# A two-layer trunk (RG-LRU, then forgetting attention): the values' bound taken from the weights, heads' operands loaded in pieces, projections reordered

## The chip, the core and the metric

The kernel runs on one core of a Trainium2 chip. A core has engines with a queue of instructions each, which run side by side and wait for one another by semaphores: TensorE (PE, matrix products; its weight loads are listed apart as PEld), VectorE (DVE), ScalarE (ACT), GpSimd (POOL) and SyncE (SP), which here only issues DMAs. The metric is the device time of one execution in microseconds.

## The reference

The input is x of 1024 tokens by 1024 channels. Two pre-norm residual layers and a final norm are computed, all in float32:

```
for i in range(2):
    h = rms_norm(x, norm_g[i])
    x = x + (lru_mixer if i == 0 else fox_mixer)(h, ...)
return rms_norm(x, final_g)

def fox_mixer(h, w_in, b_f, w_out):
    u = h @ w_in                       # q, k, v, gate: 16 heads of 64 each; f_logit: 16
    cum = cumsum(log_sigmoid(f_logit + b_f))
    logits = q @ k.T / 8 + (cum_q - cum_k), causal
    o = softmax(logits) @ v
    return (o * silu(gate)) @ w_out
```

`lru_mixer` is one product with w_in (1024 to 3072), a causal convolution over 4 tokens, two block-diagonal gates, a linear recurrence over the tokens, a SiLU gate and a product with w_out.

## The kernel before

Every product of projections takes float32 operands that are split into a high and a low part (`to_hi`, `to_lo`; `split_weights` does it for a block of weights: a load into `wf`, a cast to `wh`, a subtraction to `wl`), and runs as three matmuls: high by high, low by high, high by low. One "fill step" of a projection is six such matmuls.

The first layer runs over 12 blocks of 128 channels (loop over `n`, from line 395): per block the products with w_in, convolution, gates, recurrence; earlier blocks' output projection (`project_out`) fills in between. Lines 464 to 489 finish it: the last output projection, x written to DRAM (`x1d`), and the second norm's row sums (`rms_row`).

The second layer goes head by head. `values(g)` computes v for four heads at once (stages at g = 0, and in the runs of heads 3, 7 and 11): v is written as float16 in a high and a low part, and scaled into float16's range by a bound. `bound(g)` makes that bound: eight Squares on ACT of the weights' high parts and eight matmuls (`norms`) that sum them over the partitions, a maximum, a square root (which loads an ACT table), a reciprocal and the scales `rv`. The evacuation of v from PSUM (lines 583 and 584) uses `rv`; PSUM has two buffers for each of the tags "g", "O" and "S".

Per head, the 1024 queries are done in two chunks of 512 (c = 0, 1), and each chunk in four blocks of 128 (i). `maxima(hd, c)` yields once per block: logits S by two or four matmuls from T (keys) and U (queries), mask and row maximum on DVE, exp with row sum on ACT, the sums scaled by 1/TOP on POOL and inverted on DVE, weights in a high and a low part (`pp`, on ACT and DVE), and a DMA transpose of them to `pT`, issued by SP. `weigh(hd, c)` yields several times: O from `pT` and v.

T[s] (one tile of 1024 columns for each parity s of heads) and U are filled by DMAs on SP from the projected k and q (`load`, `load_q`): T in three large copies of 256 KB and a small one from `cumd`, U per chunk in three of 128 KB and a small one. U for c = 0 is one tile, `U0`, that all heads share.

`run(order, gens…)` writes the order out by hand: in the string, "1" is a block of `maxima`, "0" a step of `weigh`, "." a fill step of the projections for the next pair of heads (`kq_units`, `g_units`) or, for heads 12 on, of the output projection (`partial`, and then `turned`, the last part with the final norm), and each "." also advances `side`. For each head there are two runs: the first has `weigh(hd, 0)` with `maxima(hd, 1)`, the second `weigh(hd, 1)` with `maxima(hd + 1, 0)`. Heads 0 to 11 use `ORDER`, the others `LAST`. Each engine, and SP, works its queue in the order in which it was built.

Of the kernel before, what the change touches and what calls it, by code (L numbers as in the profile page):

```python
# [15 lines left out]
TOP = 32768.0  # L16
# [12 lines left out]
ORDER = "1.1.1.1..0.0", "1.1.1.1.0.00.0"  # L29
# [11 lines left out]
def trunk(ctx: ExitStack, tc: tile.TileContext, xt, w0, wg, wo0, pc, gn, gf, w1, wv, wf, bf, wo1, out):  # L41
# [11 lines left out]
    pe = [None]  # L53

# [17 lines left out]
    onesb = const.tile([P, P], BF16, name="onesb")  # L72
    nc.vector.memset(onesb, 1.0)
# [35 lines left out]
    def split_weights(src, shape, hi_eng, lo_eng, parts=wpool):  # L109
        wt = loaded(shape)  # L110
        for part, sl in src:
            nc.sync.dma_start(wt[:, :, sl], part)
# [73 lines left out]
    with ExitStack() as l0:  # L186
# [207 lines left out]

        ys, fill, held = [], iter(()), {}
        for n in range(NB):
# [66 lines left out]

        wl = [w for d0 in range(0, KT, 2) for w in out_weights(NB // 2 - 1, d0)]
        for h, cs in enumerate(halves):
# [23 lines left out]
            rms_row(sums, rs1[h], rms1[h])  # L489

# [6 lines left out]
    with ExitStack() as l1:  # L497
# [25 lines left out]
        def bound(g, parts):  # L523

            row = ps.tile([P, HALF], F32, tag="O", name="norms")[:, :256]
            for k in range(KT):
                sq = at.tile([P, 256], BF16, tag="yo", name="sqw", bufs=2)
                nc.scalar.activation(sq, f32(parts[k][0][:, :256]), AF.Square, scale=gnt[:, 1, k : k + 1])
                matmul(row, onesb, sq, start=k == 0, stop=k == KT - 1)
            most = const.tile([P, 1], F32, name=f"most{g}")  # L530
            nc.vector.tensor_reduce(most, row, mybir.AxisListType.X, ALU.max)
            nc.scalar.activation(most, most, AF.Sqrt, bias=tiny, scale=SEQ / TOP / TOP)
            unit_ = tops[g] = const.tile([P, 1], F32, name=f"unit{g}")
            nc.vector.tensor_scalar(unit_, most, 0.5 / TOP, None, ALU.mult)
            nc.vector.reciprocal(most, most)
            rv = const.tile([P, 8], F32, tag="rv", name="rv", bufs=2)
            for h in range(2):
                nc.vector.tensor_scalar(rv[:, 4 * h : 4 * h + 4], rms1[h], most, None, ALU.mult)
            return rv

        def values(g):
# [11 lines left out]
            rv = bound(g, parts)  # L553
# [5 lines left out]
            for st, k in todo:  # L559
# [19 lines left out]
                for a in range(2):  # L579
                    v = vpool.tile([P, 4, HD], FP16, tag=f"v{st}", name=f"v{st}", bufs=2)  # L580
                    src = pt[:, a * P : (a + 1) * P].rearrange("p (b d) -> p b d", b=2)
                    rv_ = rv[:, st : st + 1]
# [6 lines left out]
        tops = {}  # L589
# [8 lines left out]
        def low(pair):  # L598
            return nc.vector if pair else nc.gpsimd
# [24 lines left out]
        def load(hd, cs=slice(0, SEQ), us=(0, 1)):  # L624
# [4 lines left out]
            nc.sync.dma_start(f32(T[s][:64, 0, cs]), hi)  # L629
            nc.sync.dma_start(f32(T[s][:64, 1, cs]), hi)  # L630
            nc.sync.dma_start(f32(T[s][64:, 0, cs]), lo)
            nc.sync.dma_start(f32(T[s][66:68, 1, cs]), cumd[hd, :, cs])
            for c in us:
                load_q(hd, c)

        def load_q(hd, c):
# [3 lines left out]
            nc.sync.dma_start(f32(u[:64, 0]), hi)  # L640
            nc.sync.dma_start(f32(u[64:, 0]), hi)
            nc.sync.dma_start(f32(u[:64, 1]), lo)
            nc.sync.dma_start(f32(u[64:66, 1]), cumd[hd, :, halves[c]])
# [73 lines left out]
        def maxima(hd, c):  # L717
# [7 lines left out]
            for i in range(4 * c, 4 * c + 4):  # L725
# [6 lines left out]
                for lo_, hi_ in ((0, min(n, HALF - o_)), (HALF - o_, n)):  # L732
# [19 lines left out]
                nc.gpsimd.tensor_scalar(r, r, 1.0 / TOP, None, ALU.mult)  # L752
# [3 lines left out]
                nc.sync.dma_start_transpose(  # L756
                    turned_[:, : i + 1, :, qs].rearrange("p j t q -> p (j t) q"),
                    both.rearrange("p j t k -> p (j t k)"),
                )
                yield  # L760
        def weigh(hd, c, sub=slice(0, HALF)):
# [19 lines left out]
            to, one = yo[r0 : r0 + HD], tops[hd // 4]  # L781
# [4 lines left out]
        def gated(hd, c, sub=slice(0, HALF)):  # L786
# [10 lines left out]
            elif hd < 13:  # L797
                nc.sync.dma_start(y1d[c, pair], yo)

        def late_q(hd):  # L800
            load_q(hd, 1)
# [309 lines left out]
```

## Time and profile before

| What | us |
|---|---|
| runs: median (lowest to highest), 3 runs | 1135.74 (1133.0 to 1140.37) |
| the profiled execution's own time | 1140.27 |
| its span, first to last instruction | 1138.5 |
| PE busy | 1074.5 |
| DVE, ACT, POOL busy | 761.8, 624.9, 151.9 |
| mean granted TensorE clock | 0.975 of full speed |

The span is what the trace covers; 1.8 us of the execution's own time lie around it. "Busy" counts an instruction also while it runs at a lower clock. The first layer runs from about 6 to 464 us, the attention from about 513 to 1090 us, and the tail behind it to the end.

### The profile page before, as it was taken

To read this page: it belongs to the slowest core of one execution; us is meant where nothing else is said; L and a number is where in the kernel's file an instruction comes from. 1 tells how busy PE (TensorE), PEld (TensorE's weight loads), DVE (VectorE), ACT (ScalarE), POOL (GpSimd) and SP (SyncE) were. 2 spreads that over 40 slices of the span, in tenths; PEclk is the share of its full clock that TensorE was granted. 3 is DMA by queue.
4 is the path that set the end of the run, shared out by engine and by line. 5 is a ranking of instruction groups with operands and counts; after the bars stand their busy time and mean duration, and the time that the engine had idled before them with its cause. 6 is when DMAs were issued, how large, how long until landed. Compare 5 with 4: busy or idle time off the path is not lost. (4 is left out here: it accounts for less than half of the span.)

```text
span 1138.5 us, 14931 instructions
## 1 busy us (share of the span) xinstructions
PE 1074.5 (94%) x5130; PEld 857.5 (75%) x5130; DVE 761.8 (67%) x1314; ACT 624.9 (55%) x1053; POOL 151.9 (13%) x215
## 2 busy tenths in 40 slices
PE   9999999999999999899898899988999889999887
PEld 7788888888888887787676776767767678667666
DVE  7888765677567789558767277772776726576445
ACT  8488344445543647367656366553665536554334
POOL 1321212212021102321010000100001000011100
PEclk9999999999999999999999999998999989999899
DMA  6111111111111114338989448893588933899784
GB/s 233 56 47 50 44 52 51 47 51 42 51 52 42 51 52 144 108 95 175 165 178 191 93 114 171 180 191 87 115 177 176 190 87 90 235 210 214 180 206 184
DMA packets 212610, 138.86 MB, mean 122 GB/s; under 512 B 160660, under 2 KB 175508, under 8 KB 212536
## 3 DMA queue, kind: packets, MB, share of 16 engines
q1 hardware_dynamic: 211256, 133.73, 49.8%
q0 software_dynamic: 1280, 4.20, 1.2%
q8 instruction: 40, 0.66, 0.2%
q14 instruction: 34, 0.28, 0.1%
HBM read 59.11 MB, written 15.86 MB: 66 GB/s over the span
## 5 line engine op out<-in xcount | busy, mean ns | idle before, releaser
L56 PE MATMUL gps<-hh,wh 128*128 128x512 f32 x576 | 236.5, 411 | 1.0 <-DVE qkl L620 1.0
L56 PE MATMUL gps<-hl,wh 128*128 128x512 f32 x576 | 229.0, 397 | 0.0
L56 PE MATMUL gps<-hh,wl 128*128 128x512 f32 x576 | 228.7, 397 | 0.0
L88 ACT CAST wh<-wf 128x512 fp32r<-128x512 f32 (+2 forms) x156 | 94.1, 606 | 141.5 <-PE ops L56 53.5
L99 POOL TENSOR_TENSOR wl<-wf,wh 128x512 fp32r<-128x512 f32 (+1 forms) x60 | 99.8, 1670 | 398.5 <-ACT wh L88 367.1
L56 PEld LDWEIGHTS gps<-hl,wh 128*128 128x128 f32 x576 | 109.6, 190 | 25.7 <-issue 0.5
L56 PEld LDWEIGHTS gps<-hh,wh 128*128 128x128 f32 x576 | 110.0, 191 | 25.2 <-DVE qkl L620 1.2
L746 ACT ACTIVATE p<-S,m 128x128 f32<-128x128 f32 (+7 forms) x128 | 94.4, 738 | 59.8 <-DVE sums L753 25.1
L56 PEld LDWEIGHTS gps<-hh,wl 128*128 128x128 f32 x576 | 110.1, 191 | 20.6 <-POOL wl L99 0.3
L755 DVE SCALAR_TENSOR_TENSOR pp<-p,sums,pp 128x128 f16<-128x128 f32 (+7 forms) x128 | 104.1, 814 | 28.1 <-ACT pp L90 27.2
L90 ACT ACTIVATE pp<-p,sums 128x128 f16<-128x128 f32 (+7 forms) x128 | 97.9, 771 | 27.2 <-DVE sums L753 9.1
L741 DVE CUSTOM_DVE_ANT_0 S<-S,mask 128x128 f32<-128x128 f32 (+7 forms) x128 | 97.3, 761 | 22.5 <-PE S L56 21.0
L752 POOL TENSOR_SCALAR sums<-sums 128x1 f32<-128x1 f32 x128 | 37.8, 295 | 497.2 <-ACT p L746 497.1
L56 PE MATMUL O<-pT,v 128*128 128x512 f16 (+3 forms) x396 | 83.2, 340 | 21.5 <-DMA pT<-pp 21.5
L56 PE MATMUL S<-T,U 96*128 96x512 f32 (+7 forms) x384 | 93.7, 353 | 3.7 <-ACT p L746 3.7
L56 PE MATMUL vps<-wh,hh 128*128 128x256 f32 (+1 forms) x256 | 76.9, 301 | 15.3 <-DVE v L584 11.7
L387 DVE TENSOR_TENSOR x<-x,ops 128x512 f32<-128x512 f32 x80 | 54.1, 683 | 48.5 <-PE ops L56 48.5
L56 PEld LDWEIGHTS <-v 128*128 128x128 f16 x396 | 33.2, 102 | 68.9 <-issue 37.4
L56 PEld LDWEIGHTS S<-T,U 128*128 128x128 f32 (+1 forms) x384 | 68.8, 190 | 19.7 <-ACT p L746 6.9
L56 PE MATMUL ups<-hl,wh 128*128 128x512 f32 x192 | 76.9, 401 | 0.1
L56 PE MATMUL ups<-hh,wh 128*128 128x512 f32 x192 | 76.4, 399 | 0.6 <-ACT hh L90 0.6
L56 PE MATMUL ops<-yh,wh 128*128 128x512 f32 x192 | 76.3, 398 | 0.5 <-DVE x L480 0.5
(185 smaller groups left out, 2105.8 us busy)
## 6 DMA issues: line engine op xcount, KB each, us to landing
wf<-in_w SPq DMA_DIRECT2D x100, 256.0 KB
wf<-in_wo SPq DMA_DIRECT2D x64, 128.0 KB
U<-qkh SPq DMA_DIRECT2D x64, 128.0 KB
T<-qkh SPq DMA_DIRECT2D x28, 256.0 KB
x<-in_xt SPq DMA_DIRECT2D x16, 256.0 KB
x1d<-x SPq DMA_DIRECT2D x16, 256.0 KB
wf<-in_wv SPq DMA_DIRECT2D x16, 256.0 KB
U<-qkl SPq DMA_DIRECT2D x32, 128.0 KB
```

The lines of the kernel that those rows point to most:

```text
L56: pe[0] = nc.tensor.matmul(*args, **kw)
L88: nc.scalar.copy(hi, src)
L90: nc.scalar.activation(hi, src, AF.Copy, scale=scale)
L99: return eng.tensor_tensor(lo, src, f32(hi), ALU.subtract)
L387: nc.vector.tensor_tensor(x, x, pt, ALU.add)
L741: nc.vector.tensor_tensor_reduce(S[:, :n], S[:, :n], mask[:, SEQ - n :], -1.0, -NEG, ALU.add, ALU.min, accum_out=m)
L746: seen[0] = nc.scalar.activation(p, S[:, :n], AF.Exp, bias=m, scale=-1.0, accum_out=sums[:, i : i + 1])
L752: nc.gpsimd.tensor_scalar(r, r, 1.0 / TOP, None, ALU.mult)
L755: nc.vector.scalar_tensor_tensor(both[:, :, 1], p, r, both[:, :, 0], ALU.mult, ALU.subtract)
```

## The change

It has six parts:

1. The values' bound is made in the first layer. From block 3 on, each block loads two pieces of the raw values' weights (16 loads of 256 KB in all, `squares_of_values`), and ACT squares them with a running sum into `vsq`. `value_bounds`, behind the first half's second norm, weights these with the largest squared norm factor, sums over partitions by one matmul, and makes `scale_v`, `unit_v` and from them `rv` for all four groups of heads. `bound` goes, with its Squares, its `norms` matmuls and its square roots. (The bound is now a sum over all columns of a group, where it was the largest column.)
2. `ORDER` puts all steps of `weigh` behind the fill steps: in the second run O begins two fill steps later, in the first run one.
3. The loads of T and U0, U1 for the next heads go through `pieces`, which issues each DMA at a fill step, placed after the third-last transpose: T in two halves of 512 columns.
4. For an even head, the projections run k half 0, q half 0, k half 1 (it was k, k, q); the odd head's begin with q half 1 and then the gate. All low parts of weights there are made on DVE, also for pair 0.
5. The scaling of the sums by 1/TOP moves from POOL to DVE.
6. In `partial` the products run both halves of a block of weights one after the other from block 2 on, and the next block's weights are split at the first of the two. The residual x for the first quarter goes into T0's space in place of pT0's, and the result into pT0.

`fetch` is SP's DMA start, as before.

```diff
-ORDER = "1.1.1.1..0.0", "1.1.1.1.0.00.0"
+ORDER = "1.1.1.1...00", "1.1.1.1...0000"
...
+        def squares_of_values():
+            for g, i in itertools.product(range(4), range(4)):
+                wt = loaded((2, 256))
+                nc.sync.dma_start(wt, wv[g, :, 2 * i : 2 * i + 2])
+                flat = wt.rearrange("p a b -> p (a b)")
+                nc.scalar.activation(flat, flat, AF.Square, accum_out=vsq[:, g, i : i + 1])
+                yield
...
+            if n > 2:
+                take(vsquares, 2)
...
+        def value_bounds():
+            g2 = const.tile([P, KT], F32, name="g2")
+            nc.vector.tensor_tensor(g2, gnt[:, 1], gnt[:, 1], ALU.mult)
+            g2 = g2.rearrange("p (k two) -> p k two", two=2)
+            most = const.tile([P, 4], F32, name="most")
+            nc.vector.tensor_tensor(most, g2[:, :, 0], g2[:, :, 1], ALU.max)
+            nc.vector.tensor_tensor(vsq, vsq, most.unsqueeze(1).to_broadcast([P, 4, 4]), ALU.mult)
+            all_ = ps.tile([P, 16], F32, tag="O", name="vnorm")
+            matmul(all_, onesf, vsq.rearrange("p a b -> p (a b)"), start=True, stop=True)
+            nc.vector.tensor_reduce(
+                scale_v, all_.rearrange("p (a b) -> p a b", b=4), mybir.AxisListType.X, ALU.add
+            )
+            nc.scalar.activation(scale_v, scale_v, AF.Sqrt, bias=tiny, scale=SEQ / TOP / TOP)
+            nc.vector.tensor_scalar(unit_v, scale_v, 0.5 / TOP, None, ALU.mult)
+            nc.vector.reciprocal(scale_v, scale_v)
...
-            rv = bound(g, parts)
...
+        def piece(to, src):
+            with tc.issue_after(turns[-3].ins):
+                fetch(to, src)
+
+        def pieces(hd, is_k, c):
+            if hd >= HEADS:
+                return
+            pair, s = hd // 2, hd % 2
+            rows, cs = slice(s * HD, (s + 1) * HD), halves[c]
+            hi, lo = (f32(z[rows, cs]) for z in kq[pair, is_k])
+            if is_k:
+                t, cs_ = T[s], cs
+                todo = (t[:64, 0, cs], hi), (t[:64, 1, cs], hi), (t[64:, 0, cs], lo), (t[66:68, 1, cs], cumd[hd, :, cs])
+            else:
+                t = U[s][c]
+                todo = (t[:64, 0], hi), (t[64:, 0], hi), (t[:64, 1], lo), (t[64:66, 1], cumd[hd, :, cs])
+            for to, from_ in todo:
+                piece(f32(to), from_)
+                if to is not todo[2][0]:
+                    yield
...
-                nc.gpsimd.tensor_scalar(r, r, 1.0 / TOP, None, ALU.mult)
+                nc.vector.tensor_scalar(r, r, 1.0 / TOP, None, ALU.mult)
...
-                if c:
+                if c if db < 2 else not c:
                     split_out(db + 1)
...
-                xs = at.tile([P, KT, 256], F32, tag="pT0", name="x1", bufs=1)
+                xs = tu.tile([P, KT, 256], F32, tag="T0", name="x1")
...
-                    fill = kq_units(pair + 1, ((1, (0, 1)), (0, (0,))))
+                    fill = kq_units(pair + 1, ((1, (0,)), (0, (0,)), (1, (1,))))
...
-                    pairs = ((0, 1), (2, 3), (4, 5), (6, 7))
-                    todo = [(db, c) for two in pairs for c in range(2) for db in two]
+                    todo = [(db, c) for c in range(2) for db in range(2)]
+                    todo += [(db, c) for db in range(2, KT) for c in range(2)]
...
-                fill = chain(kq_units(pair + 1, ((0, (1,)),)), late_q(hd + 1), g_units(pair + 1))
+                fill = chain(kq_units(pair + 1, ((0, (1,)),)), g_units(pair + 1))
...
-            run(first, weigh(hd, 0), maxima(hd, 1), fill=fill)
+            side = chain(pieces(hd + 1, 0, 0), pieces(hd + 1, 1, 1)) if hd else iter(())
+            run(first, weigh(hd, 0), maxima(hd, 1), fill=fill, side=side)
+            drain(side)
...
-            side = late() if hd == 14 else iter(())
+            side = pieces(hd + 2, 1, 0)
+            if hd:
+                side = chain(pieces(hd + 1, 0, 1), side)
...
-            if hd + 2 < HEADS:
-                load(hd + 2, us=(0,) if hd % 2 == 0 and hd < 12 else (0, 1))
```

Three places show what moves in the queues. Numbers behind names are those of buffers.

PE before, in head 1's second run, from the last S of head 2's chunk 0 to the first product O of head 1's chunk 1 (`gps1` is a projection):

```order
L56 MATMUL S_4474<-T1_3569,U_3570 128x512 x2
L56 MATMUL gps1_4467<-hh_3281,wh_4457 128x512
L56 MATMUL gps1_4467<-hh_3281,wl_4458 128x512
L56 MATMUL gps1_4467<-hl_3282,wh_4457 128x512
L56 MATMUL gps1_4467<-hh_3283,wh_4457 128x512
L56 MATMUL gps1_4467<-hh_3283,wl_4458 128x512
L56 MATMUL gps1_4467<-hl_3284,wh_4457 128x512
L56 LDWEIGHTS v0_3763
L56 MATMUL O_4494<-pT_4269,v0_3763 128x512
```

The same place after the change (the line left out stands for 15 more rows of `gps1_4498`):

```order
L60 MATMUL S_4507<-T1_3632,U_3633 128x512 x2
L60 MATMUL gps1_4498<-hh_3483,wh_4318 128x512
L60 MATMUL gps1_4498<-hh_3483,wl_4319 128x512
...
L60 MATMUL gps1_4498<-hl_3494,wh_4324 128x512
L60 LDWEIGHTS v0_3792
L60 MATMUL O_4539<-pT_4298,v0_3792 128x512
```

Six matmuls stood between the last S and O, and now 18 do.

ACT before, at the second value stage (`sqw` are the Squares of `bound`, `most1` its square root, `v0` the first evacuation of v):

```order
L710 ACTIVATE sg1_5158<-gps1_5265 128x512
L528 ACTIVATE sqw_5343<-wh_5199,gnt_95 128x256
...
L528 ACTIVATE sqw_5361<-wh_5335,gnt_95 128x256
L532 ACT_TABLE_LOAD
L532 ACTIVATE most1_5364<-most1_5364,tiny_78 128x1
L90 ACTIVATE v0_5411<-vps_5373,rv_5370 128x2x64
```

After the change (`yo` is the evacuation of O):

```order
L90 CAST wh_5380<-wf_5378 128x512
L92 ACTIVATE pp_5320<-p_5318,sums_5246 128x4x128
L759 ACTIVATE sg1_5192<-gps1_5304 128x512
L833 ACTIVATE yo_5075<-O_5348,unit_v_3297 64x512
L92 ACTIVATE v0_5422<-vps_5384,rv_3296 128x2x64
L92 ACTIVATE v0_5425<-vps_5384,rv_3296 128x2x64
```

The Squares, the table load and the square root no longer stand ahead of v's evacuation.

SP before, around the transposes of head 3's chunk 1 (`U0_3571` is head 4's own U for c = 1 and `T1_3569` the keys of head 5; `wf` the values' weights):

```order
L756 DMA_TRANSPOSE pT_5065<-pp_5075 128x10x128
L112 DMA wf_5333<-in_wv 128x512
L630 DMA T1_3569<-qkh_4814 64x1024
L756 DMA_TRANSPOSE pT_5065<-pp_5097 128x12x128
L631 DMA T1_3569<-qkl_4815 64x1024
L640 DMA U0_3571<-qkh_4982 64x512
L756 DMA_TRANSPOSE pT_5065<-pp_5118 128x14x128
L756 DMA_TRANSPOSE pT_5065<-pp_5139 128x16x128
```

The same place after the change (`U_3633` is the shared U0 with head 4's queries, `T0_3631` the keys of head 4):

```order
L806 DMA_TRANSPOSE pT_5098<-pp_5108 128x10x128
L57 DMA U_3633<-qkl_4932 64x512
L57 DMA U_3633<-cumd_3624 2x512
L57 DMA wf_5378<-in_wv 128x512
L806 DMA_TRANSPOSE pT_5098<-pp_5131 128x12x128
L57 DMA T0_3631<-qkh_4839 64x512 x2
L57 DMA T0_3631<-qkl_4840 64x512
L806 DMA_TRANSPOSE pT_5098<-pp_5153 128x14x128
L806 DMA_TRANSPOSE pT_5098<-pp_5176 128x16x128
```

The shared U0's low part and its piece from `cumd`, which were issued ahead of chunk 1's first transpose, now follow it, and the keys' copies are half as large.

More of the change, by code (lines that the diff above doesn't have):

```diff
@@ L111, in split_weights @@
         for part, sl in src:
-            nc.sync.dma_start(wt[:, :, sl], part)
+            fetch(wt[:, :, sl], part)
         hi = parts.tile([P, *shape], F32R, tag="wh", name="wh")
@@ L489, in trunk @@
             rms_row(sums, rs1[h], rms1[h])
+            if h == 0:
+                value_bounds()
+            nc.vector.tensor_tensor(
+                rv[:, :, 4 * h : 4 * h + 4],
+                rms1[h].unsqueeze(1).to_broadcast([P, 4, 4]),
+                scale_v.unsqueeze(2).to_broadcast([P, 4, 4]),
+                ALU.mult,
+            )
     y1d = dram.tile([2, KT, P, HALF], F32, name="y1d")
@@ L521, in project @@
                 use(h, pt)
[L523 to L539, printed above, removed]
         def values(g):
@@ L598, in low @@
         def low(pair):
-            return nc.vector if pair else nc.gpsimd
+            return nc.vector
         def kq_units(pair, parts=((1, (0, 1)), (0, (0, 1)))):
@@ L894, in turned @@
             if c == 0:
-                res = tu.tile([P, 2, SEQ], F32, tag=f"T{q}", name="res")
+                if q:
+                    res = tu.tile([P, 2, SEQ], F32, tag="T1", name="res")
+                else:
+                    res = at.tile([P, 2, SEQ], F32, tag="pT0", name="res", bufs=1)
                 res = [res[:, b] for b in range(2)]
@@ L1011, in trunk @@
             gated(hd, 0)
-            side = late() if hd == 14 else iter(())
+            side = pieces(hd + 2, 1, 0)
+            if hd:
+                side = chain(pieces(hd + 1, 0, 1), side)
+            if hd == 14:
+                side = chain(side, late())
             if hd % 4 == 3 and hd < 12:
```

55 lines of the change are left out of this document (30 added, 25 removed).

## The prediction

> **What bounds the kernel now.** The first view is the page's list of engines, with two stretches of the view by windows beside it (columns there: window, its length, busy time of PE, PEld, DVE, ACT and POOL with instruction counts, granted clock, DMA share, GB/s).
>
> ```profile
> PE 1074.5 (94%) x5130; PEld 857.5 (75%) x5130; DVE 761.8 (67%) x1314; ACT 624.9 (55%) x1053; POOL 151.9 (13%) x215
> ```
>
> ```profile
> 20.00:420.00 400.00, 400.00 (x1726) 324.14 (x1725) 295.75 (x322) 215.25 (x257) 76.35 (x44) 1.00 0.15 48
> 517.00:625.00 108.00, 100.19 (x467) 76.25 (x466) 82.44 (x181) 69.20 (x133) 10.22 (x34) 0.98 0.92 179
> ```
>
> PE is the bound. In the first layer it has no gap in 400 us, at clock 1.00, so nothing can be gained there; in the attention it stands still for 7.8 of 108 us, beside a DMA share of 0.92. Time can come back only from PE's waits, from matmuls that go, or from matmuls at half clock. So the view of waits comes second, cut to PE (waited for: total us, times, longest).
>
> ```profile
> PE O L56 <- DMA pT<-pp: 21.5, 10, 3.6
> PE vps L56 <- DVE v L584: 11.7, 3, 3.9
> PE ops L56 <- ACT wh L88: 5.5, 1, 5.5
> PE turn L56 <- DMA x<-x1d: 4.5, 1, 4.5
> PE S L56 <- ACT p L746: 3.7, 4, 1.7
> PE vps L56 <- DVE fz L587: 3.6, 1, 3.6
> PE ops L56 <- DVE sg L711: 2.3, 1, 2.3
> PE norms L56 <- ACT sqw L528: 1.5, 4, 0.5
> ```
>
> The change touches all but S and the second ops: O behind the transposed weights, v behind its evacuation (which waits for the bound), and two in the tail. Third, what follows such a wait: the window after one O wait, and the one behind it.
>
> ```profile
> 570.00:573.40 3.40, 3.40 (x10) 1.95 (x9) 0.60 (x1) 0.00 (x0) 0.00 (x0) 0.50 0.61 146
> 573.40:576.00 2.60, 2.60 (x14) 1.61 (x13) 0.00 (x0) 0.00 (x0) 0.00 (x0) 1.00 0.90 171
> ```
>
> PE counts as busy in both, but at 0.50 it did 10 matmuls in 3.40 us, at 1.00 14 in 2.60 (0.186 each): the ten were worth 1.9 us, so 1.5 us are lost behind the wait (1.7 by the clock alone). A wait costs its length and this tail.
>
> **The change, part by part.** Sums are made against the profiled execution, 1140.27 us; the median of the runs is 1135.74, so 4.5 is taken off at the end.
>
> *The values' bound.* The stretch after the second value stage's stall, from the time line and two windows:
>
> ```profile
> 649.03 0.55 PE L56 MATMUL vps<-wh,hh 128*128 128x256 f32 x1 [3.90 <-DVE v L584]
> ```
>
> ```profile
> 649.00:651.90 2.90, 2.87 (x13) 2.90 (x14) 0.66 (x3) 0.27 (x2) 0.00 (x0) 0.50 0.04 8
> 651.90:655.00 3.10, 3.10 (x28) 3.10 (x27) 0.70 (x2) 0.73 (x2) 0.00 (x0) 1.00 0.00 0
> ```
>
> In the changed order v's evacuation on ACT has no Square, table load or Sqrt ahead of it, and its scale is a constant made in the first layer. So the waits 11.7 + 3.6 + 1.5 = 16.8 us go. The 32 norms matmuls (8 in each of four stages) go too, at 3.10 / 28 = 0.11 us a place: 3.5. Behind each of four stalls 13 matmuls took 2.90 us that were worth 1.44: 1.4 × 4 = 5.8. Together **26**. What is late next is v's own evacuation, which at the unstalled places keeps two PSUM buffers ahead of PE; nothing is charged.
>
> Its price is in the first layer: 16 loads of 256 KB and 16 Squares with a sum. The nearest rows are the norm's Square of the same size and the reading of an accumulator after the exponentials:
>
> ```profile
> L169 ACT ACTIVATE sq<-x 128x512 f32<-128x512 f32 x16 | 9.9, 618 | 1.1 <-DVE yl L99 1.1
> ```
>
> ```profile
> L746 ACT ACTIVATION_READ_ACCUMULATOR p<-S,m 128x1 f32 x128 | 24.6, 192 | 0.0
> ```
>
> 16 × (0.618 + 0.192) = 13 us on ACT. They lie beside PE's 400 us, in which ACT has 185 us free and DMA is used at 0.15. If that cover fails at every place, 13 us; a gain is excluded, as PE has no gap there. They stand mid-stage, in front of the casts that PE waits for next, so I take 1, near the idle end. `value_bounds` itself is one 16-column matmul on PE and some six small instructions on DVE and ACT beside the output projection: between 0 and 2 us (six at the size of the 0.192 above and the Sqrt's), taken 0.5.
>
> *v's products last.* O at c = 1 (in the second run of a head) now comes after two more fill steps. A row of the chain has such a step, six matmuls of 0.23 us:
>
> ```profile
> 955.48 1.39 PE gps L56 x6
> ```
>
> So the transposes get 2.8 us more (at c = 0, one step). Of the ten waits six are of 2.5 us and more (the other four under 0.9). The first, the third and the last of the six, from PE's time line:
>
> ```profile
> 569.03 0.39 PE L56 MATMUL O<-pT,v 128*128 128x512 f16 x1 [3.56 <-DMA pT<-pp]
> ...
> 710.40 1.87 PE L56 MATMUL O<-pT,v 128*128 128x512 f16 x4 [2.65 <-DMA pT<-pp]
> ...
> 908.82 0.61 PE L56 MATMUL O<-pT,v 128*128 128x512 f16 x1 [3.34 <-DMA pT<-pp]
> ```
>
> ```profile
> 710.40:713.30 2.90, 2.90 (x7) 1.72 (x8) 0.77 (x2) 0.69 (x1) 0.00 (x0) 0.50 0.73 186
> ```
>
> What is longer than 2.8 us stays: 0.76 of the first, 0.54 of the last, 2.3 us over the six. So 19.2 of 21.5 go. Six stretches at half clock, 1.5 each, are 9.2. If the transposes land when they do now, that is 28; the changed loads stand between them, so I leave a third of the half clock's gain (3) and 4 us of waits, and take **21.5**, with 28 and 0 as the ends.
>
> [...]
>
> *The tail.* Rows of SP's queue, of PE and of the chain, then windows:
>
> ```profile
> 1043.89 7.93 SPq L756 DMA_TRANSPOSE pT<-pp  x2
> ```
>
> ```profile
> 1056.54 0.80 PE L56 MATMUL ops<-yhh,wh 128*128 128x512 f32 x1 [5.55 <-ACT wh L88]
> ```
>
> ```profile
> 1098.73 1.14 PE L56 MATMUL turn<-ident,x 128*128 128x128 f32 x3 [4.52 <-DMA x<-x1d]
> ```
>
> ```profile
> 1095.17 3.51 DMA x<-x1d
> ```
>
> ```profile
> 1056.50:1061.50 5.00, 4.96 (x12) 3.83 (x13) 3.17 (x9) 2.51 (x6) 0.80 (x2) 0.50 0.48 109
> 1098.70:1102.40 3.70, 3.67 (x12) 2.50 (x13) 0.05 (x1) 0.47 (x1) 0.00 (x0) 0.55 0.92 271
> ```
>
> The next weight's load follows these two transposes, at 1051.9, and stalls PE 5.5 us; x's loads are issued at 1095.17, after the last transpose, and stall it 4.5. The new `todo` splits weights a product earlier, ahead of head 14's transposes, and x goes to T0, free before pT0, so its loads are issued from head 14's transposes on. Half clock behind them: 12 matmuls worth 12 × 0.23 = 2.8 us took 5.0 (2.2 lost) and 3.7 (0.9). 5.5 + 4.5 + 3.1 = 13.1; the last load still follows the last transposes, so I take **11** (0 to 13.1).
>
> *Operands in pieces.* Per head, T comes as eight issues of 128 KB and less in place of four, and half of U0 is now queued behind the first transpose of chunk 1. Rows of SP by line (ns min/median/max) and of the time line of head 1:
>
> ```profile
> L756 SPq DMA_TRANSPOSE pT<-pp x128: 1173/1505/4631, 518.1 to 1090.8; - x128
> ```
>
> ```profile
> L630 SPq DMA_DIRECT2D T<-qkh x18: 466/584/1066, 462.3 to 1000.6; - x18
> ```
>
> ```profile
> L641 SPq DMA_DIRECT2D U<-qkh x32: 461/588/1167, 468.0 to 1019.9; - x32
> ```
>
> ```profile
> 545.76 0.85 PE L56 MATMUL S<-T,U 128*128 128x320 f32 x4
> ```
>
> ```profile
> 558.37 0.49 PE L56 MATMUL S<-T,U 128*128 128x256 f32 x2
> ```
>
> ```profile
> 553.60 1.66 SPq L756 DMA_TRANSPOSE pT<-pp  x1
> ```
>
> The next head's first S is due 12.6 us after chunk 1's first S; that transpose is issued at +7.8 for 1.66 us, U0's two pieces behind it at 0.59 each end at +10.7, and land by the 3.51 us above at about +14, or, with only their own 0.59 more, at +11.3. Between 0 and 1.6 us late in each of 14 heads: 0 to 22, taken 5, because the page's 3.51 held seven loads and this is two.
>
> *The rest.* Sums on DVE: the operation goes into the queue of the engine that waits for it; 128 at the accumulator's 0.19 are 25 us, on an engine busy 82.44 of 108, and they replace the 25.8 of the next row, so 0 (±5). Reordered projections: a weight split has four fill steps ahead of it where some had eight; uncovered it costs 12 casts, and as many subtractions taken at the cast's size, 24 × 0.616 = 15, taken 1 (a gain is possible only in PE's waits, counted above).
>
> ```profile
> DVE sums L753 <- POOL sums L752: 25.8, 37, 1.8
> ```
>
> ```profile
> L88 ACT CAST wh<-wf 128x512 fp32r<-128x512 f32 x144 | 88.3, 616 | 128.4 <-PE ops L56 51.0 <-PE gps L56 38.9 <-issue 19.8
> ```
>
> Sum: 26 + 21.5 + 11 = 58.5 gained, 1 + 0.5 + 5 + 1 = 7.5 lost, net 51. 1140.3 − 51 = 1089.3, less 4.5: **1085**.
>
> **Rivals.** *Everything lands:* 26 + 28 + 13 = 67 and nothing is lost: 1069. For it: each cost has a cover in the rows.
>
> *SP's queue takes O's gain.* SP issues about eight transposes (8 × 1.5 = 12.0), four T (2.3) and eight U loads (4.7) per head, 19 of the 28 us that lie between 569.03 and 624.94 for two heads. The rows of T (256 KB, 584 ns) and U (128 KB, 588 ns) say that a load's issue costs the same whatever its size, so halving T adds 4 × 0.59 = 2.4 per head. Half of it stands ahead of chunk 1's last transposes: 12 × 1.2 = 14 us of O waits come back, and with them the half clock that I counted (6): 1105. [...]
>
> *Slower: U0 late in every head.* If the DMA engines (0.92) bring U0's pieces behind the transpose's own traffic, S waits at the start of each of 14 second runs. To end over 1% slower, they must eat 56 and 11 more, 67 / 14 = 4.8 each, 3.3 of wait and 1.5 of half clock: landing at +15.9, 5.2 after their issue. At 6.5 it would be 14 × 6.1 = 85: 1085 + 80 = 1165. For it: transposes whose issue took 4.6 us; against: 3.51 for seven loads at a DMA share of 0.92.
>
> *The first layer pays.* 13 us of Squares and late weights uncovered, and 14 of the 15 for splits: 1085 + 27 = 1112. Against: ACT is free for 46% of that stage. *The waits only move*, from O to S or to splits, so that part 2 and the pieces do nothing: 1085 + 21.5 = 1107.
>
> **How the numbers follow.** Forecast 0.49 (its own range 1075 to 1095), everything lands 0.10, SP's queue 0.15, first layer 0.07, waits only move 0.05, U0 late 0.14. A measurement of this kernel tells about 1% (11 us) from no change. All but the last are faster by more: 0.86. U0 late is spread over 1107 to 1165, by how late it is: 0.01 still faster, 0.05 within 1%, 0.08 slower. So faster 0.87, same 0.05, slower 0.08. The range reaches from 1064 (all gains, and 5 us below for the spread of the runs) to 1113, just past the first layer's case; outside it lies U0's case and little else.
>
> **What the new profile would show.** Right: no wait of vps for v, no norms; O waits below 6 us in all; no half clock at the value stages; ops and turn waits under 2 us; S waits below 8. SP's queue: O waits of 14 us or more with transposes issued after loads of T. U0: a wait of S for U after each first run. First layer: PE under 400 busy in that stretch, with a wait for wh. Wrong above all if S, which hardly waits now, waits in every head.

## The result, and the profile after

The changed kernel takes 1104.78 us (median of 4 runs, 1101.88 to 1107.29) against 1134.37 us for the kernel before (1129.94 to 1140.37, 4 runs): a ratio of 0.9735, 95% interval 0.9682 to 0.9788. That is 30 us faster, inside the whole range of the forecast (1064 to 1113) and on its side, but the likeliest case had 50 us, and the forecast's own 1075 to 1095 is missed. The profiled execution takes 1107.29 us (span 1105.5) beside 1140.27 before: 33.0 us less, where the sum had 51.

The engines in the page of the changed kernel, and the head of its view of waits, cut to PE:

```profile
PE 1057.9 (96%) x5100; PEld 849.1 (77%) x5100; DVE 777.4 (70%) x1439; ACT 613.3 (55%) x1044; POOL 100.3 (9%) x77
```

```profile
PE S L60 <- DMA U<-cumd: 10.4, 8, 2.0
PE O L60 <- DMA pT<-pp: 8.6, 5, 3.3
PE S L60 <- ACT p L795: 7.5, 6, 2.4
PE gps L60 <- DVE qkl L101: 2.7, 4, 1.2
PE turn L60 <- DVE xp L915: 2.4, 1, 2.4
```

v's and the norms' waits are gone, and O waits 8.6 us where it waited 21.5. At the top stands a wait that was not there before: S for the last piece of U. PE's idle time (span less busy time) fell from 64.0 to 47.6 us, and its busy time by 16.6 us. About 3.5 us of that are the norms' matmuls, by the forecast's price for them; most of the rest are matmuls that no longer run at half clock (mean granted clock 0.975 before, 0.991 after).

Where the time went shows best by stage. Windows of before, then of after (window, length, busy of PE and its count, PEld, DVE, ACT, POOL, granted clock, DMA share, GB/s): from the first product of v to the first S of the attention or of the next head's chunk 1, for the four value stages, and then from head 12's chunk 1 to the end.

```profile
460.15:511.68 51.53, 47.36 (x299) 42.41 (x298) 25.10 (x58) 24.73 (x49) 13.85 (x13) 0.97 0.33 91
631.99:661.76 29.77, 25.52 (x203) 24.80 (x202) 9.68 (x26) 12.83 (x29) 0.00 (x0) 0.94 0.28 72
773.95:803.95 30.00, 25.74 (x204) 25.02 (x203) 9.70 (x26) 12.84 (x29) 0.00 (x0) 0.94 0.22 61
917.20:947.64 30.44, 26.18 (x204) 25.47 (x202) 9.70 (x26) 12.84 (x29) 0.00 (x0) 0.89 0.20 55
947.64:1138.50 190.86, 169.57 (x796) 130.67 (x794) 113.47 (x234) 92.22 (x186) 17.05 (x44) 0.96 0.78 197
```

```profile
465.44:510.73 45.29, 44.57 (x291) 40.40 (x290) 26.63 (x60) 22.86 (x40) 5.79 (x7) 1.00 0.42 110
627.74:650.67 22.93, 22.93 (x195) 22.93 (x194) 7.42 (x18) 7.48 (x18) 0.00 (x0) 1.00 0.41 99
759.65:782.57 22.92, 22.92 (x195) 22.92 (x194) 7.71 (x19) 7.48 (x18) 0.00 (x0) 1.00 0.42 107
889.10:912.03 22.93, 22.93 (x195) 22.93 (x194) 7.89 (x19) 7.48 (x18) 0.00 (x0) 1.00 0.46 114
912.03:1105.50 193.47, 169.92 (x796) 130.00 (x794) 117.08 (x262) 90.93 (x185) 8.84 (x16) 0.97 0.80 198
```

The bounds of these windows give a balance of the whole kernel, in us, profiled execution against profiled execution:

| Stretch | Before | After | Difference | Forecast |
|---|---|---|---|---|
| first layer, to the first product of v | 460.15 | 465.44 | +5.3 | +1.5 |
| four value stages | 141.74 | 114.07 | −27.7 | −26 |
| heads between them | 345.75 | 332.52 | −13.2 | −16.5 and +1 for the rest |
| from head 12's chunk 1 to the end | 190.86 | 193.47 | +2.6 | −11 |
| sum | 1138.50 | 1105.50 | −33.0 | −51 |

In the value stages of heads 3, 7 and 11 PE has no gap left, at clock 1.00. The tail, which was to gain 11 us, lost 2.6; the first layer paid 5.3.

**The first layer** pays at one place. PE's time line there, ACT's a little ahead of it, and the window:

```profile
104.08 0.50 PE L60 MATMUL ups<-hh,wh 128*128 128x512 f32 x1 [1.68 <-ACT wh L90]
...
105.96 0.80 PE L60 MATMUL ups<-hh,wl 128*128 128x512 f32 x1 [0.92 <-POOL wl L101]
```

```profile
94.93 0.63 ACT L405 ACTIVATE wf<-wf 128x512 f32<-128x512 f32 x1 [0.76 <-DMA wf<-in_wv]
...
98.91 0.63 ACT L405 ACTIVATE wf<-wf 128x512 f32<-128x512 f32 x1 [0.78 <-DMA wf<-in_wv]
```

```profile
100.00:112.00 12.00, 9.34 (x32) 6.69 (x32) 10.45 (x9) 11.87 (x14) 5.09 (x2) 0.86 0.22 70
```

These are the third and fourth Squares in ACT's queue; the first two ran at 50.98 and 55.47. Each waits a little for its load, ACT is then busy 11.87 of the 12 us from 100 on, the two casts behind the Squares end at 104.5 (in the kernel before, at 100.3), PE waits 1.68 + 0.92 us and then runs partly at half clock (0.86 in the window, 0.50 from 105.9 to 108.9). PE does not wait at the other 14 Squares, though the one at 133.92 waits 4.96 us for its load. So it is not the wait for a load by itself that costs, but where this pair stands in ACT's queue: ahead of casts that PE needs next.

**The pieces.** SP's queue in head 1's second run, and the S of head 2's chunk 1 that needs what it loads:

```profile
569.93 0.58 SPq L57 DMA_DIRECT2D U<-qkh  x1
570.61 1.28 SPq L806 DMA_TRANSPOSE pT<-pp  x1
571.94 0.58 SPq L57 DMA_DIRECT2D U<-qkl  x1
572.57 0.43 SPq L57 DMA_DIRECT2D U<-cumd  x1
```

```profile
574.85 0.69 PE L60 MATMUL S<-T,U 96*128 96x320 f32 x3 [2.00 <-DMA U<-cumd]
```

Here it is head 2's own U for chunk 1, not the shared U0: its low part and its piece of the sums are queued behind three transposes of head 2's chunk 0, and land 2.0 us after S needs them. Eight of the heads wait like this, 0.6 to 2.0 us each.

The copies also hold what they read from. ACT, which evacuates the next pair's k and q into the tiles that T and U are copied from, stands still 12.0 us in all ahead of those evacuations until copies have landed (11 waits); in the kernel with whole loads (below) no such wait is among the 60 largest sums of its view of waits (3.4 us and more).

**The tail.** Head 14's second run, SP, ACT and PE:

```profile
1017.09 4.64 SPq L806 DMA_TRANSPOSE pT<-pp  x1
1021.78 0.59 SPq L57 DMA_DIRECT2D U<-qkh  x1
```

```profile
1026.53 0.62 ACT L90 CAST woh<-wf 128x512 fp32r<-128x512 f32 x1 [6.78 <-DMA pT<-pp]
```

```profile
1025.80 0.82 PE L60 MATMUL O<-pT,v 128*128 128x512 f16 x3 [3.33 <-DMA pT<-pp]
```

ACT stands still 6.78 us ahead of a cast of late weights. The cast's tile is the one from which head 15's U is copied (the code gives them one tag, `qkh0`), and a copy of U is issued only at 1021.78, behind 4.64 us of a transpose. The profile names a transpose of the same queue as the last to land; that it is the copy is argued from the code. Behind the cast stand two exponentials of head 15, and PE's O waits for transposes in the meantime.

### The profile page after: what moved, and what is told of

Its sections match the earlier page's. It is cut to its first block, busy times and chain, and to the rows that moved or that the text cites. A ratio compares the mean times of both kernels' runs of the same rounds, so it can differ in the third digit from the quotient of the medians.

```text
span 1105.5 us, 14905 instructions
## 1 busy us (share of the span) xinstructions
PE 1057.9 (96%) x5100; PEld 849.1 (77%) x5100; DVE 777.4 (70%) x1439; ACT 613.3 (55%) x1044; POOL 100.3 (9%) x77
## 5 line engine op out<-in xcount | busy, mean ns | idle before, releaser
L60 PE MATMUL gps<-hh,wh 128*128 128x512 f32 x576 | 228.5, 397 | 2.7 <-DVE qkl L101 2.7
L101 POOL TENSOR_TENSOR wl<-wf,wh 128x512 fp32r<-128x512 f32 (+1 forms) x50 | 86.6, 1740 | 379.1 <-ACT wh L90 272.8
L60 PE MATMUL S<-T,U 96*128 96x512 f32 (+7 forms) x384 | 96.4, 357 | 20.2 <-DMA U<-cumd 10.4
L101 DVE TENSOR_TENSOR wl<-wf,wh 128x512 fp32r<-128x512 f32 x106 | 70.2, 666 | 19.0 <-ACT wh L90 18.7
L60 PE MATMUL O<-pT,v 128*128 128x512 f16 (+3 forms) x396 | 71.3, 322 | 8.7 <-DMA pT<-pp 8.6
L60 PE MATMUL ups<-hh,wl 128*128 128x512 f32 x192 | 77.2, 402 | 0.9 <-POOL wl L101 0.9
L60 PE MATMUL ops<-yh,wl 128*128 128x512 f32 x192 | 75.7, 394 | 0.1
```

The costliest lines, as they stand in the source:

```text
L60: pe[0] = nc.tensor.matmul(*args, **kw)
L101: return eng.tensor_tensor(lo, src, f32(hi), ALU.subtract)
```

## The experiments

Each kernel ran beside the kernel before on the same chip (medians of before 1132.0 to 1132.9 us there). Ratios are to the kernel before, with 95% intervals. Two changed kernels are compared by their medians, some of which come from different chips, so differences of a few us between them can't be told.

### One part alone: v's products last

```diff
-ORDER = "1.1.1.1..0.0", "1.1.1.1.0.00.0"
+ORDER = "1.1.1.1...00", "1.1.1.1...0000"
```

> The kernel before with part 2 alone (the two strings of ORDER). Theory: O's products only lacked time, so with 2.8 us more the ten O waits of 21.5 us fall to under 4 us and the half clock behind six of them goes: 25 us less, about 1109; the loads stay as before, so the wait of S for U that the changed kernel shows (10.4 us) does not come up. Rival: the waits only move, to S or to the evacuation of O, and less than half is kept: 1122 or more.

Measured: 1113.42 us, ratio 0.9808 (0.9761 to 0.9855), 19 us less. Its waits of PE for O:

```profile
PE O L56 <- DMA pT<-pp: 4.5, 5, 1.8
```

21.5 us became 4.5, almost as the theory had it. The gain lies between its 25 and the rival's 11: S's waits for exponentials grew from 3.7 to 6.6 us and the norms' from 1.5 to 3.4, so some of the time moved. The forecast's 21.5 us for this term was about right.

### One part alone: the values' bound

```diff
+        def squares_of_values():
...
+        def value_bounds():
...
-            rv = bound(g, parts)
```

> The kernel before with part 1 alone (the values' bound from the weights, made in the first layer). Theory: the four value stages shrink by 6 to 7.5 us each as in the changed kernel (27.7 in all), and the first layer loses 5.0 us at one place, near 104 us, where the first two Squares hold up the casts of block 3's weights: 22 us less, about 1112. Rival: the stages' gain hangs on the other parts (what comes behind the value stage waits in their place): under 12 us, 1122 or more.

Measured: 1107.33 us, ratio 0.9762 (0.9706 to 0.9819), 25.5 us less. The theory's 22 is met and the rival is out. Part of what goes beyond it lies in the tail, which takes 185.8 us in place of 190.9 although this edit leaves the tail's order alone. This part alone is worth nearly as much as the whole change; in its trace the first layer pays the same 5.2 us, and O waits 24.1 us:

```profile
PE O L56 <- DMA pT<-pp: 24.1, 12, 4.3
```

### Undoing part 6: the tail's order

```diff
-                if c if db < 2 else not c:
+                if c:
...
-                    todo = [(db, c) for c in range(2) for db in range(2)]
-                    todo += [(db, c) for db in range(2, KT) for c in range(2)]
+                    pairs = ((0, 1), (2, 3), (4, 5), (6, 7))
+                    todo = [(db, c) for two in pairs for c in range(2) for db in two]
```

(and x and the result in their tiles of before)

> The changed kernel without part 6 (order of the output projection's products, and x and the result in their old tiles). Theory: part 6 does take away the two waits of before (5.5 and 4.5 us and their half clock, 13 us), and the new waits of the tail (17.6 us from head 12's chunk 1 on) come from the pieces and not from part 6, so undoing it costs about 11: 1115. Rival: part 6's earlier splits and loads of weights, which stand ahead of the exponentials on ACT, and of the transposes on SP, cause the new waits; then undoing it costs nothing: 1100 to 1106.

Measured: 1111.4 us, ratio 0.9788 (0.974 to 0.9836): 6.6 us more than the changed kernel, between 11 and nothing. In this kernel PE waits 4.1 us for x and 4.0 us for weights again. But of the 5.5 us between the two traces only about 3 lie in the tail (196.4 us from head 12's chunk 1 to the end, against 193.5), and 2.5 stand ahead of it, where the two kernels are the same. So part 6 is worth some 3 to 7 us here, less than was forecast, and the tail's new waits are not its doing alone.

### Undoing part 3: loads in pieces

```diff
-            side = chain(pieces(hd + 1, 0, 0), pieces(hd + 1, 1, 1)) if hd else iter(())
-            run(first, weigh(hd, 0), maxima(hd, 1), fill=fill, side=side)
-            drain(side)
+            run(first, weigh(hd, 0), maxima(hd, 1), fill=fill)
...
+            if hd + 2 < HEADS:
+                load(hd + 2, us=(0,) if hd % 2 == 0 and hd < 12 else (0, 1))
```

(and `late_q` back in the odd heads)

> The changed kernel without part 3 (heads' operands loaded whole, and where before loaded them). Theory: the eight waits of S for U's last piece (10.4 us) go, and with them the 6.8 us for which ACT waits in head 14's second run to cast a late weight into a tile that head 15's U1 is still copied from, and PE's 3.3 us behind it; O keeps its room: 12 us less than the changed kernel, about 1093. Rival: the whole copies in front of the transposes make O late again by more than the 2.8 us it has: 1104 or more.

Measured: 1087.61 us, ratio 0.9583 (0.9537 to 0.9628): **17 us faster than the changed kernel**. The rival is out, and the gain is 5 us more than the theory's. Its PE waits, and its window from head 12's chunk 1 to the end:

```profile
PE O L60 <- DMA pT<-pp: 12.4, 8, 2.3
PE S L60 <- ACT p L795: 8.6, 8, 2.5
```

```profile
901.78:1088.08 186.30, 166.71 (x796) 128.97 (x794) 117.67 (x262) 90.69 (x185) 8.84 (x16) 0.97 0.80 202
```

No S waits for U. O waits 12.4 us, more than in the changed kernel's 8.6, so the pieces did give O some room; but it costs far more. The tail takes 186.3 us in place of 193.5. The profiled execution is 50.4 us shorter than that of before: the forecast's sum for the rest of the change, without its 5 for the pieces, has 56. So part 3 is where most of the missing time went: 17 us lost where the sum had 5, which is 12 of the 20 us between the likeliest time and the measured one.

Parts 1 and 2 alone gave 25.5 and 19.4 us, together 44.9; the kernel without part 3 is 45.2 us below the kernel before. By this sum parts 4, 5 and 6 add nothing to it. Parts 1 and 2 together, without the others, were not run.

### Halves or place: whole place, T in two halves

```diff
+            for h in (halves if cs == slice(0, SEQ) else (cs,)):
+                hi, lo = (f32(z[rows, h]) for z in kq[pair, 1])
+                fetch(f32(T[s][:64, 0, h]), hi)
...
```

(on the kernel without part 3; the same four copies for each half)

> The changed kernel with the loads where they were before the change (as in the run that undid part 3), but T in two halves of 512 columns: four more issues per head and nothing else. Theory: place, not number, made the pieces dear: within 3 us of that run, 1085 to 1091. Rival (the one on SP's queue in the prediction): the four more issues, 2.4 us per head, come on the last transposes of a head: 12 x 1.2 us, 1098 or more.

Measured: 1093.45 us, ratio 0.9656 (0.9618 to 0.9695): 5.8 us more than with whole copies. Neither theory holds in full: over the 14 heads that are loaded so, four more issues cost 0.4 us per head, not 0 and not 1.2. And they do not come on O:

```profile
PE S L60 <- ACT p L797: 11.6, 8, 2.2
PE O L60 <- DMA pT<-pp: 5.6, 4, 1.9
```

O waits less (5.6 against 12.4 us), S for exponentials more (11.6 against 8.6). What is longer beside S are small waits, above all those of the projections for weights (4.4 us in place of 0.9), and 2.2 us of PE's busy time. By subtraction about a third of part 3's price is number and the rest is place; that the two add up was not shown.

### U's copies earlier

```diff
-        def piece(to, src):
-            with tc.issue_after(turns[-3].ins):
+        def piece(to, src, back=3):
+            with tc.issue_after(turns[-back].ins):
...
-                piece(f32(to), from_)
-                if to is not todo[2][0]:
+                early = not is_k and c
+                piece(f32(to), from_, 5 if early else 3)
+                if early:
+                    if to is todo[1][0] or to is todo[3][0]:
+                        yield
+                elif to is not todo[2][0]:
```

> The changed kernel with U1's four copies issued earlier: two each at the first two fill steps, and placed after the fifth-last transpose in place of the third-last; T stays in halves, U0 as it was. Theory: the waits of S for U (10.4 us) come from U1's low part and its piece from the sums being queued behind three transposes of the next chunk; with one or two of them ahead they go, and the tail (7 us worse than with whole loads) stays or gains a little: 1093 to 1097. Rival: the sheer number of issues and bytes in SP's queue delays whatever comes last in it, so the wait only moves to T, to U0 or to O: 1101 or more.

Measured: 1115.28 us, ratio 0.9847 (0.9803 to 0.989): 10.5 us *more* than the changed kernel. The theory falls, the rival holds: the wait moves. The head of its PE waits, and one of the new ones, followed back from PE to DVE, ACT and SP:

```profile
PE gps L60 <- DVE qkl L101: 11.5, 4, 4.0
PE S L60 <- DMA U<-cumd: 9.7, 6, 2.2
```

```profile
593.15 0.80 PE L60 MATMUL gps<-hh,wh 128*128 128x512 f32 x1 [4.03 <-DVE qkl L101]
```

```profile
592.40 0.69 DVE L101 TENSOR_TENSOR qkl<-gps,qkh 128x512 fp32r<-128x512 f32 x1 [0.48 <-DMA T<-qkl]
```

```profile
586.85 0.59 ACT L90 CAST qkh<-gps 128x512 fp32r<-128x512 f32 x1 [1.82 <-DMA T<-qkh]
```

```profile
584.91 4.61 SPq L810 DMA_TRANSPOSE pT<-pp  x2
589.57 0.58 SPq L57 DMA_DIRECT2D T<-qkl  x1
```

U's copies went ahead of T's, and T's copies read the tiles into which the next pair's k is evacuated. ACT stood still 1.82 us ahead of the high part's evacuation (`qkh`) until two of them had landed, and pushed back the exponentials behind it. T's last copy was issued behind two transposes at 589.57, and DVE stood still 0.48 us more for it ahead of the low part's (`qkl`). Only then was the PSUM buffer free for which PE waited, 4.03 us in all; what is left of these is other work in DVE's and ACT's queues, and the shares were not separated. So a late copy held its source here (these 1.82 and 0.48 us) as well as its target (S's 9.7 us for U).

### U in pieces, T whole

```diff
-            side = chain(pieces(hd + 1, 0, 0), pieces(hd + 1, 1, 1)) if hd else iter(())
+            side = pieces(hd + 1, 0, 0) if hd else iter(())
...
-            side = pieces(hd + 2, 1, 0)
-            if hd:
-                side = chain(pieces(hd + 1, 0, 1), side)
+            side = pieces(hd + 1, 0, 1) if hd else iter(())
...
+            if hd + 2 < HEADS:
+                load(hd + 2, us=())
```

> The changed kernel with U0 and U1 in pieces as in the change, but T loaded whole, at the end of each second run as before the change. Of the 17 us that part 3 costs in the changed kernel (1104.8 against 1087.6 without it), theory: most belongs to U, whose last pieces are queued behind transposes of the run that precedes their use; so the S waits for U (10.4 us) stay and T's return gains 6 at most, as the run with T in halves lost 6: 1098 to 1104. Rival: T's six pieces among the transposes are what makes U late (they use SP and the DMA engines); with T out of the way U lands in time: 1088 to 1092.

Measured: 1115.51 us, ratio 0.9859 (0.9811 to 0.9908): 10.7 us more than the changed kernel, outside what either theory had. The wait of S for U doubles, and now comes at the start of both chunks:

```profile
PE S L60 <- DMA U<-cumd: 23.4, 15, 2.4
```

```profile
553.17 0.47 SPq L57 DMA_DIRECT2D T<-qkh  x1
553.74 1.74 SPq L806 DMA_TRANSPOSE pT<-pp  x1
555.53 1.03 SPq L57 DMA_DIRECT2D U<-qkl  x1
556.65 1.38 SPq L806 DMA_TRANSPOSE pT<-pp  x1
558.09 0.98 SPq L57 DMA_DIRECT2D U<-cumd  x1
```

```profile
560.79 0.35 PE L60 MATMUL S<-T,U 96*128 96x256 f32 x1 [2.04 <-DMA U<-cumd]
```

This is the U0 that the prediction feared: its last piece is issued at 558.09, behind two transposes. (In the changed kernel the same piece goes out at 555.01, behind one, and S does not wait for it.) So U placed between transposes is dear by itself: 28 us against the kernel with all loads whole. And T's pieces are not needed to make U late; with T whole ahead of it in the queue, U comes later still. Which of SP's issues and the DMA engines' traffic sets the delay was not separated.

### Undoing part 4: the projections' order

```diff
-                    fill = kq_units(pair + 1, ((1, (0,)), (0, (0,)), (1, (1,))))
+                    fill = kq_units(pair + 1, ((1, (0, 1)), (0, (0,))))
```

(the order alone; the low parts of weights stay on DVE)

On the changed kernel:

> The changed kernel without part 4 (k in both halves first, then q half 0). Theory: the order of the projections is worth nothing by itself, as PE does the same products and no wait for weights shows: 1101 to 1108. Rival: it is what lets U0's copies start in time in the first run; without it they come two groups of fill steps (11 us) later for every second head, and S waits at the start of six second runs by 3 us and more: 1120 or more.

Measured: 1113.78 us, ratio 0.9823 (0.9776 to 0.987): 9 us more. Neither number is met; the direction is the rival's. Then the same edit on the kernel without part 3 (and with the Squares moved, next section):

> The kernel without part 3 and with the Squares from block 4 on (1085.0), also without part 4. Theory: part 4 was worth 9 us to the changed kernel because U0's and T's pieces read the projections' tiles at fixed fill steps; with whole loads at a head's end its order does not matter: 1083 to 1088. Rival: it pays by itself, as q's first half and its evacuation then lie away from a head's end: 1092 or more.

Measured: 1085.34 us, ratio 0.9585 (0.9544 to 0.9625), against 1084.98: nothing. The theory holds: part 4 is worth 9 us only as a servant of the pieces.

### The Squares from block 4 on

```diff
-            if n > 2:
+            if n > 3:
                 take(vsquares, 2)
```

(on the kernel without part 3)

> The changed kernel without part 3, and with the Squares of the values' weights from block 4 on in place of block 3. Theory: the first layer's 5.0 us come from block 3 alone, where ACT waits for the first two loads of values' weights while the casts of block 3's second weights are due; block 4 has room as the later blocks have: 1082.6. Rival: it is the first pair, wherever it stands, and the stall moves to block 4: 1087.

Measured: 1084.98 us, ratio 0.9586 (0.9543 to 0.9628), 2.6 us less than without the move; the two overlap in their runs. The trace is plainer, and not as either text has it. The pair that cost was never the first but the second, block 4's, near 95 us. With the move the first pair falls away and this one is pulled apart: its Squares now run at 94.76 and 107.24, the second behind the two casts (101.76). PE's waits for weights near 104 us are gone, none has come up elsewhere, and from 20 to 420 us PE is busy 399.9 us where it was 397.6 without the move. So the first layer's price was that place alone.

### Undoing part 5: the sums' scaling

```diff
-                nc.vector.tensor_scalar(r, r, 1.0 / TOP, None, ALU.mult)
+                nc.gpsimd.tensor_scalar(r, r, 1.0 / TOP, None, ALU.mult)
```

(on the kernel of the last section)

> The same kernel (1085.0) without part 5: the sums' scaling on POOL again. Theory: the 25.8 us in which DVE waited for POOL lie beside O's room now, so little is lost, but O still waits 13 us in that kernel for transposes that end a chain through this step (0.5 us longer per block with POOL), so 2 to 6 us: 1087 to 1091. Rival: DVE is the tighter engine and is relieved of 128 operations: 1082 or less.

Measured: 1081.25 us, ratio 0.955 (0.9513 to 0.9586), 3.7 us less than with the scaling on DVE: the rival's number, and the theory's 1087 to 1091 is missed, though the difference is so near to what can be told that part 5 is only shown not to help. O's waits are much the same (12.9 against 13.4 us). The theory's 0.5 us per block was its author's estimate: the operation itself takes 0.21 us on POOL in the kernel before and 0.15 on DVE in the changed kernel, and DVE waited for POOL at 37 of the 128 blocks, 0.7 us each on average.

### v's products last in the last four heads too

```diff
-LAST = "1..1..1.1..0.0.", "1..1..1.1.0..0.0..0"
+LAST = "1..1..1.1....00", "1..1..1.1......0000"
```

(on the kernel with whole loads and the Squares from block 4 on, sums on DVE)

> The same kernel (1085.0) with v's products last in the last four heads too (LAST as 1..1..1.1....00 and 1..1..1.1......0000). Theory: the O waits of heads 12 to 14 (1.6 us and what the exponentials wait behind them) go, nothing else is late: 1081 to 1084. Rival: the tail is bound by DVE and ACT there, so S waits by as much and O's later evacuation delays the gate and the last products: 1086 or more.

Measured: **1078.66 us** (1077.93 to 1081.13), ratio 0.9529 (0.9492 to 0.9566), 6.3 us less than without it and 26 less than the changed kernel: the fastest kernel run here. Its window from head 12's chunk 1 to the end, beside the 186.3 and 193.5 above:

```profile
897.12:1077.40 180.28, 164.88 (x796) 129.34 (x794) 117.87 (x262) 90.67 (x185) 8.83 (x16) 0.98 0.81 208
```

(The kernel without this edit has 189.4 in its trace, which is of the slowest of its four runs.) The gain is more than the theory's, and O's waits are not where it comes from: the one named, 1.6 us, is gone, but O waits 13.1 us in all where it waited 13.4. PE's waits in the tail fall from 13.8 to 9.4 us, most of it the first wait of `turn` for DVE (`xp`, the sum of x and a product), 0.3 in place of 3.4. The kernel that joins this with the scaling on POOL was not run.

## Why the prediction was right, and where its sum was off

The direction and the whole range held, and of the reasons the ones that carry the gain; the likeliest time was 20 us too fast. The range held by its width: 1104.8 lies outside the forecast's own 1075 to 1095 and beside two rivals, 1105 and 1107, neither of which came about as it was told. Of the signs that the prediction named for itself, those of the value stages came true (no waits for v and the norms, clock 1.00). Three did not: O waited 8.6 us (below 6 was named), S 20 (below 8), `turn` 3.2 (under 2). And S, the sign of being wrong above all, waited for U in eight heads. By its own steps:

- **What bounds the kernel** was right. PE's waits, the half clock behind them and the norms' matmuls were what there was to gain: the change took 16.4 us of idle time and 16.6 of busy time.
- **The values' bound**, 26 us: 27.7 in the trace. The count of waits, matmuls and half clock was sound term by term.
- **Its price in the first layer**, taken as 1 of a bound of 13 us: about 5 at one place, and none elsewhere. The bound was put on all 16 Squares; what cost was one pair of them ahead of two casts that PE needed next. The step had seen such casts and priced them near nothing; that one late pair also brings half clock behind PE's waits (0.50 behind the 1.68 and 0.92 us) was not in it.
- **v's products last**, 21.5 us: 19 us when done alone, with O's waits at 4.5 us. Right within what can be told; in the whole change O waits 8.6 us.
- **The pieces**, taken as 5 of a bound of 22: this step failed, in size and in place. The prediction looked at U0, behind the first transpose of chunk 1. In the changed kernel the wait came at each chunk 1's own U, behind three transposes of chunk 0; of it the prediction said nothing. Nor did it ask what else a late copy holds: ACT's 12.0 us ahead of evacuations. Undoing part 3 gives 17 us back. The rival on SP's queue saw that pieces are dear, and at 1105 its time is the measured one, but by chance and not by its mechanism: the four more issues cost 5.8 us in place of 20, and not at O.
- **The tail**, 11 us: the two waits named were taken away, but new ones of the same size came, and part of them came through the pieces: the tail takes 190.9 to 196.4 us in the five kernels that have any, 184.4 to 189.4 in the five with the loads in their old place and the old `LAST`, and 190.9 before. How much part 6 itself takes is not settled: with the values' bound alone, the tail's order untouched, the weights' wait of 5.5 us is already down to 1.7. The sum had counted waits that go and not asked what DVE, ACT and SP do there when PE no longer stands still; this last is argued.
- **The projections' order** and **the sums**, 1 and 0: part 4 is worth 0 without the pieces and 9 us with them; part 5 costs perhaps 4.
- **Half clock behind a wait** was counted at all six O waits of 2.5 us and more, from rows at two of them. The trace of before bears it out: in windows of 2.9 to 3.0 us behind the six (2.51 to 3.56 us) the granted clock was 0.50 to 0.69. In another kernel it did not follow every such wait (last section).

## What to carry to other kernels

Here loads strewn among the transposes in SP's queue were late: S waited 10.4 us for U's last piece, 2.0 of it at the place shown, where three transposes stood in front, and ACT stood still 12.0 us until copies had landed out of the tiles that it writes next. Operands loaded whole were 17 us cheaper; where a load must be split, count for each piece the issues ahead of it up to its use, and ask who writes its source next. When a change removes waits, take each of its parts away again by itself: here one part of six cost 17 us and the others hid it. A product that waits for a long chain of other engines was cheaper here when placed last, behind the work that needs nothing from them (19 us in the first twelve heads, some 6 in the last four).

## What the runs showed of the hardware that was not expected

Whether the granted clock fell behind a wait did not follow from the wait's length alone. In the kernel with the values' bound alone, O waits of 3.16, 2.36 and 3.16 us, and the windows behind them (the granted clock is the third number from the end):

```profile
622.98 0.60 PE L56 MATMUL O<-pT,v 128*128 128x512 f16 x2 [3.16 <-DMA pT<-pp]
...
698.77 0.59 PE L56 MATMUL O<-pT,v 128*128 128x512 f16 x2 [2.36 <-DMA pT<-pp]
...
889.67 0.60 PE L56 MATMUL O<-pT,v 128*128 128x512 f16 x2 [3.16 <-DMA pT<-pp]
```

```profile
623.20:626.20 3.00, 3.00 (x15) 1.82 (x14) 0.75 (x1) 0.56 (x1) 0.00 (x0) 1.00 1.11 165
698.80:701.80 3.00, 3.00 (x10) 1.82 (x10) 1.03 (x2) 0.67 (x1) 0.00 (x0) 0.71 0.77 189
...
889.80:892.80 3.00, 3.00 (x14) 1.74 (x13) 0.75 (x1) 0.65 (x1) 0.00 (x0) 1.00 0.74 184
```

Behind the 2.36 us wait the granted clock was 0.71 in the window, behind the two of 3.16 us it was 1.00. What decides it no run here shows.
